# One plain chunk per feed-forward block in place of two, and the first pair's p1 and p2 among its products

## The chip, the cores and the metric

The kernel runs on one core of a Trainium2 chip. The time is the device time of one execution in microseconds (us); the median of three runs before the change is 2769.42 us (2768.85 to 2770.11). Smaller is better. Five engines work side by side, each through its own list of instructions: TensorE (PE, matrix products), VectorE (DVE), ScalarE (ACT), GpSimd (POOL) and SyncE (SP, which starts most of the loads). An instruction starts when the one ahead of it on its engine has been started and when what it reads is there.

## The reference

Two requests, of 512 and 256 tokens of 1024 numbers, go through an encoder of two layers with the same weights. Each layer is half a feed-forward block, a token mixer, and half a feed-forward block. The first layer's mixer is a gated linear recurrence in both directions, the second's is attention in a window of 128 tokens. A norm closes the trunk. The change concerns the feed-forward blocks alone, of which there are four, called f0 to f3 here:

```python
def rmsnorm(x, g):
    return x * lax.rsqrt(jnp.mean(x * x, axis=-1, keepdims=True) + NORM_EPS) * g

def swiglu_ffn(x, w1, w2):           # w1: 1024 x (2 * 2816), w2: 2816 x 1024
    gate, up = jnp.split(x @ w1, 2, axis=-1)
    return (jax.nn.silu(gate) * up) @ w2

x = x + 0.5 * swiglu_ffn(rmsnorm(x, g0), w1[0], w2[0])
x = x + mixer(rmsnorm(x, g1))
x = x + 0.5 * swiglu_ffn(rmsnorm(x, g2), w1[1], w2[1])
```

## The kernel before

All 768 tokens are handled together, as two halves of 384 (`H`). The 2816 hidden columns are 22 chunks of 128 (`NF`).

**Products in three parts.** Each fp32 operand is split in a high part (ACT rounds it by a cast) and a low part (DVE subtracts the high part from the source), in `split`. A product of two operands is then three matmuls: high by high, high by low, low by high. In `mm3` these are lines 314, 315 and 316. So the first of the three needs only the high part of the activations, the second needs their low part.

**Plain chunks and pairs.** A *plain* chunk computes gate and up by themselves: for each half, 8 slices of the input columns x 3 matmuls for the gate product, and as many for the up product, 96 matmuls in all (`up_plain`). A *pair* (`up_pair`) computes the 2 x 2 block product of (gate, up) by (first half, second half) with seven products instead of eight, p1 to p7, each 4 slices x 3 matmuls: 84 matmuls, all recorded on line 513. The price is that its operands are sums of quarters. The activations have four quarters, b00, b10, b01 and b11; the first digit is the half of the input columns (k 0 to 3, or k 4 to 7), the second is the half of the tokens. p1 uses b00, p2 uses b10, p3 uses b11. p4, p5, p6 and p7 use the factors t4, t1, t2 and t3, which are differences of quarters, formed once a block by `sums` (through `mix`, DVE lines 422, 423, 433 and 434) and split by `put` (ACT line 319, DVE line 320). The weights have sums of the same kind: POOL's queue starts accumulating DMAs for some (`into`), DVE adds others (line 215), ACT casts them (line 208 for pairs, 175 for plain chunks), and DVE makes their low parts (lines 209 and 176). Only the low part of p5's weight is made by POOL.

**A block.** Before the change, chunks 0 and 1 of each block are plain, chunks 2 to 21 are pairs. Four chunks together (two *kp* of two) make a group; their hidden values, after Silu and product, go through a seven-product scheme too, in `down_quad` (line 577). The last two chunks use plain down products.

**Entry of a block.** The normed activations must be turned so that columns lie on partitions. `turn(half, part)` does it: transposes on PE (line 385), scaled evictions on ACT (line 396), then `put` splits the quarter. The first half is turned ahead of the block. Turning the second half and forming the factors are put in a queue of steps by `later`, and `run_later` takes a step off at certain slices of the plain chunks, so these matmuls stand while the operands of the pairs are made.

**Order.** The program is written engine by engine by a scheduler that takes the order of the code as priority and sets each engine's list when the kernel is built. Weight tiles lie in pools (4 raw, 8 split), and `ahead` stages the next weights as soon as tiles come free.

Of the kernel before, what the change touches and what calls it, by code (L numbers as in the profile page):

```python
# [16 lines left out]
P = 128  # L17
# [19 lines left out]
PLAIN = 2  # L37
# [6 lines left out]
UP = ("p1", "p7", "p2", "p5", "p4", "p6", "p3")  # L44
TOK = ("p1", "p2", "p7", "p6", "p5", "p4", "p3")
# [7 lines left out]
class Trunk:  # L53
# [385 lines left out]
    def sums(self):  # L439
        for kp in range(2):  # L440
            tiles = (self.tn[(i // 2, i % 2)][:, kp] for i in range(4))
            self.mix(*tiles, lambda name, src: self.put(name, kp, src))
# [80 lines left out]
    def up_pair(self, tag, j):  # L523
        nc = self.nc
        key = (tag, j)
        a, b, c, d = (self.ps(H) for _ in range(4))
        v, w, t = (self.tmp(H) for _ in range(3))
        p = lambda name, ps, first, last: self.product(key, name, FACTOR[name], ps, first, last)
        p("p1", a, True, False)
        nc.scalar.copy(v, a)  # L530
        self.ahead()
# [3 lines left out]
        p("p2", a, False, True)  # L535
        nc.scalar.activation(a, a, AF.Silu)
        self.ahead()
# [18 lines left out]
    def down_quad(self, tag, g, hid):  # L556
        nc = self.nc
        cols = lambda b, c: self.x[b][:, c * 512 : (c + 1) * 512]
        if g == 0:
            for i in range(HB):  # L560
                x12, x21, x22 = cols(HB + i, 0), cols(i, 1), cols(HB + i, 1)
                nc.vector.tensor_add(x12, x12, x22)
                nc.vector.tensor_sub(x21, x21, x22)
# [37 lines left out]
    def ffn(self, tag, next_row):  # L601
        for g in range(GROUPS):
# [10 lines left out]
            if g == 0:  # L613
                ts = {}
                for half in range(2):
                    for j in range(PLAIN):
                        t = ts[2 * j + half] = self.up_plain(tag, j, half)
                        name = f"b{j}{half}"
                        if name != "b01":
                            put(name, t, 0)  # L620
                gather(ts, 0)
                self.run_later(len(self.deferred))
            for kp in range(2):
                if g == 0 and kp == 0:
                    continue
                ts = []
                for j in range(2):
# [932 lines left out]
```

## Time and profile before

| | |
|---|---|
| median of 3 runs | 2769.42 us |
| profiled execution, span | 2767.2 us |
| PE busy | 2745.0 us, 99%, 15117 instructions |
| DVE busy | 2206.5 us, 80%, 3766 instructions |
| ACT busy | 1386.0 us, 50%, 2589 instructions |
| POOL busy | 453.0 us, 16%, 491 instructions |
| line 513, pairs | 6720 matmuls, 1169.3 us |
| lines 314 to 316, 384 columns | 1920 matmuls, 649.9 us |
| line 577, down products | 2520 matmuls, 575.7 us |

The times of runs include some 2 us around the span that the profile shows. A row of a group gives line, engine, operation, output and inputs, the count, then busy time in us and the mean in ns, then the idle time just before and what ended it. A row of a timeline gives the start and the length in us. In the chain of waits each row is a stretch of the work that ended last. Matmuls overlap in the records: one of 384 columns is listed with 0.33 us or more, while the starts are 0.17 us apart.

### The profile page before, as it was taken

The numbers are of one execution on the slowest core, as the hardware profiler recorded it, in microseconds if no ns is written. First come the engines' busy times: TensorE is split into PE (matmuls) and PEld (weight loads), VectorE is DVE, ScalarE is ACT, GpSimd is POOL, SyncE is SP. The second block draws the span as 40 slices with busy tenths as digits, with TensorE's granted clock in tenths as the row PEclk, the third lists the DMA queues.
The fourth block names the chain that finished last, engine by engine and source line by source line (L and its number), as shares of the span: only waits on it lengthen the run. The fifth ranks groups of instructions, "written<-read, shape, count | busy, mean of one in ns | idle before, by whom it ended". The sixth has DMA issues, their size and how long they took to land.

```text
span 2767.2 us, 40933 instructions
## 1 busy us (share of the span) xinstructions
PE 2745.0 (99%) x15117; PEld 2554.8 (92%) x15117; DVE 2206.5 (80%) x3766; ACT 1386.0 (50%) x2589; POOL 453.0 (16%) x491
## 2 busy tenths in 40 slices
PE   8999999999999999999999999999999999999998
PEld 8999999989999889999999999999888889999998
DVE  8788788767887888788878887887847868788877
ACT  7344444634455675444445543444458855444443
POOL 2111121200000101211111121111105611211111
PEclk9999999999999999999999999999999999999999
DMA  6554554851122743655444355544424422655443
GB/s 172 130 125 114 126 140 124 227 161 39 39 62 66 205 119 78 143 134 131 115 117 121 78 145 134 126 119 118 130 73 111 89 69 73 145 134 130 114 118 107
DMA packets 352040, 325.22 MB, mean 118 GB/s; under 512 B 14216, under 2 KB 271200, under 8 KB 351840
## 3 DMA queue, kind: packets, MB, share of 16 engines
q1 hardware_dynamic: 303040, 224.56, 27.7%
q0 software_dynamic: 44496, 84.56, 17.4%
q10 hardware_dynamic: 4304, 13.49, 1.3%
q8 instruction: 118, 1.93, 0.3%
q14 instruction: 82, 0.67, 0.1%
HBM read 225.82 MB, written 15.73 MB: 87 GB/s over the span
## 4 chain that ended last, share of the span: by engine, by line
PE 96%; DVE 2%; ACT 1%; DMA 1%; issue 0%; DVEq 0%; POOL 0%; SPq 0%; ACTq 0%; POOLq 0%
PE ps L513 42%; PE ps L577 21%; PE ps L315 6%; PE ps L316 6%; PE ps L314 6%; PE ps L760 5%; PE ps L823 3%; PE ps L928 1%; PE ps L1414 1%; PE ps L904 1%; PE ps L385 1%; PE ps L1426 0%; PE ps L1376 0%; PE ps L1427 0%; PE ps L1377 0%; PE ps L1181 0%
## 5 line engine op out<-in xcount | busy, mean ns | idle before, releaser
L513 PE MATMUL ps<-big,w 128*128 128x384 f32 x6720 | 1169.3, 334 | 0.0
L513 PEld LDWEIGHTS ps<-big,w 128*128 128x128 f32 x6720 | 1165.9, 188 | 1.7 <-ACT tA L530 0.2
L208 ACT CAST w<-wr 128x512 fp32r<-128x512 f32 x600 | 415.8, 707 | 689.2 <-PE ps L513 274.9
L577 PE MATMUL ps<-w,big 128*128 128x512 f32 x2520 | 575.7, 390 | 0.0
L577 PEld LDWEIGHTS ps<-w,big 128*128 128x128 f32 x2520 | 472.7, 188 | 98.0 <-ACT big L319 0.4
L209 DVE TENSOR_TENSOR w<-wr,w 128x512 fp32r<-128x512 f32 (+1 forms) x520 | 438.0, 846 | 145.9 <-ACT w L208 123.9
L147 POOL DMA_DIRECT2D s<-wr x126 | 109.8, 878 | 1250.3 <-DMA s<-in_ffn_w_dram 432.0
L599 DVE SCALAR_TENSOR_TENSOR x<-ps,x 128x512 f32<-128x512 f32 x468 | 302.4, 686 | 10.1 <-PE ps L316 10.0
L314 PE MATMUL ps<-big,w 128*128 128x384 f32 x640 | 219.6, 345 | 1.2 <-ACT w L175 0.9
L315 PE MATMUL ps<-big,w 128*128 128x384 f32 x640 | 215.7, 337 | 0.7 <-DVE big L320 0.7
L316 PE MATMUL ps<-big,w 128*128 128x384 f32 x640 | 214.6, 335 | 0.0
L319 ACT CAST big<-tA 128x384 fp32r<-128x384 f32 x296 | 148.0, 513 | 115.4 <-DVE tA L545 37.0
L147 POOL DMA_DIRECT2D wr<-wr x109 | 94.9, 871 | 518.3 <-DMA wr<-in_ffn_w_dram 165.9
L760 PE MATMUL ps<-w,big 128*128 128x512 f32 x756 | 177.1, 392 | 0.1
L320 DVE TENSOR_TENSOR big<-tA,big 128x384 fp32r<-128x384 f32 x296 | 168.0, 578 | 6.7 <-ACT big L319 4.7
L209 POOL TENSOR_TENSOR w<-wr,w 128x512 fp32r<-128x512 f32 x80 | 137.4, 1718 | 197.8 <-ACT w L208 195.8
L760 PEld LDWEIGHTS ps<-w,big 128*128 128x128 f32 x756 | 140.6, 188 | 29.1 <-DVE w L320 0.6
L215 DVE TENSOR_TENSOR wr<-wr,wr 128x512 f32<-128x512 f32 (+1 forms) x120 | 123.3, 1027 | 25.9 <-issue 23.6
L314 PE MATMUL ps<-w,big 128*128 128x512 f32 x336 | 134.6, 401 | 0.1
L316 PE MATMUL ps<-w,big 128*128 128x512 f32 x336 | 131.8, 392 | 0.5 <-DVE big L400 0.5
L315 PE MATMUL ps<-w,big 128*128 128x512 f32 x336 | 131.8, 392 | 0.0
L315 PEld LDWEIGHTS ps<-big,w 128*128 128x128 f32 x640 | 120.6, 188 | 2.0 <-DVE big L320 1.7
(214 smaller groups left out, 3504.0 us busy)
## 6 DMA issues: line engine op xcount, KB each, us to landing
wr<-in_ffn_w_dram SPq DMA_DIRECT2D x264, 512.0 KB, 4.0
s<-wr POOLq DMA_DIRECT2D x126, 256.0 KB, 4.8
s<-in_ffn_w_dram SPq DMA_DIRECT2D x120, 256.0 KB, 3.2
wr<-wr POOLq DMA_DIRECT2D x80, 256.0 KB, 3.8
wr<-in_hg_w_in_dram SPq DMA_DIRECT2D x32, 512.0 KB, 3.9
wr<-wr POOLq DMA_DIRECT2D x29, 512.0 KB, 4.6
spill<-x ACTq DMA_DIRECT2D x12, 512.0 KB, 4.0
kept<-big POOLq DMA_DIRECT2D x8, 768.0 KB, 9.7
```

The costliest lines, as they stand in the source:

```text
L147: self.nc.gpsimd.dma_start(out, src, accum_op=ALU.add)
L208: nc.scalar.copy(h, src)
L209: (eng or nc.vector).tensor_sub(l, src, h.bitcast(F32))
L314: nc.tensor.matmul(out, a[0], b[0], start=first, stop=False)
L315: nc.tensor.matmul(out, a[0], b[1], start=False, stop=False)
L316: nc.tensor.matmul(out, a[1], b[0], start=False, stop=last)
L319: self.nc.scalar.copy(hi, src)
L320: self.nc.vector.tensor_sub(lo, src, hi.bitcast(F32))
L513: self.nc.tensor.matmul(ps, a[x], b[y], start=first and k == 0 and i == 0, stop=k == 3 and i == 2, skip_group_check=True,)
L577: nc.tensor.matmul(ps, a[x], w[y], start=name == chain and kp == 0 and q == 0, stop=kp == 1 and q == 2, skip_group_check=True,)
L599: self.nc.vector.scalar_tensor_tensor(x, ps, c, x, ALU.mult, ALU.add)
L760: nc.tensor.matmul(ps, x[:, sl], y, start=fresh and k == 0 and q == 0, stop=k == 3 and q == 2, skip_group_check=True,)
```

## The change

Each block has one plain chunk (`PLAIN = 1`), and chunk 1 becomes the second member of a first pair of chunks, computed with seven products. For the first half of the tokens, the block does the plain chunk's gate product, then p1 of chunk 1, then the plain chunk's up product (with `run_later` at its slices 2 and 6), then p2 of chunk 1, then what is left of the queue of steps, the sums. The plain chunk's second half follows, and then p7, p5, p4, p6 and p3. The weights of that chunk are staged in this order (`UP_OPEN`). `sums` forms each factor over both halves of the columns before it forms the next: t3, t1, t2's difference, t4, and t2's split last. The six additions on x ahead of the first down product (lines 562 and 563 before) are held until the first pair's last DVE instruction. At the last down products the weights are released without staging ahead each time; that is done once behind them.

```diff
-PLAIN = 2
+PLAIN = 1
+UP_OPEN = ("p1", "p2", "p7", "p5", "p4", "p6", "p3")
...
     def sums(self):
-        for kp in range(2):
-            tiles = (self.tn[(i // 2, i % 2)][:, kp] for i in range(4))
-            self.mix(*tiles, lambda name, src: self.put(name, kp, src))
+        b11, b12, b21, b22 = (self.tn[(i // 2, i % 2)] for i in range(4))
+
+        def form(name, t, a, b):
+            for kp in range(2):
+                self.nc.vector.tensor_sub(t[:, kp], a[:, kp], b[:, kp])
+            return lambda: [self.put(name, kp, t[:, kp]) for kp in range(2)]
+
+        form("t3", b22, b12, b22)()
+        form("t1", b12, b11, b12)()
+        t2 = form("t2", b11, b11, b22)
+        form("t4", b21, b21, b11)()
+        t2()
...
-                self.plan_quad((tag, i), (gate, up), (NC, P), UP)
+                self.plan_quad((tag, i), (gate, up), (NC, P), UP_OPEN if i == PLAIN else UP)
...
-    def up_plain(self, tag, j, half):
+    def up_plain(self, tag, j, half, between=None):
         pss = []
         for c in range(2):
+            if c and between:
+                between()
             wh, wl = self.take((tag, j, c))
...
-                if half == 0 and k in (((), (2, 6)), ((3, 7), (3, 7)))[j][c]:
+                if half == 0 and c and k in (2, 6):
                     self.run_later()
...
+    def up_first(self, tag, j):
+        a, v = self.ps(H), self.tmp(H)
+        self.product((tag, j), "p1", FACTOR["p1"], a, True, False)
+        self.nc.scalar.copy(v, a)
+        self.ahead()
+        return a, v
+
+    def up_second(self, tag, j, a):
+        self.product((tag, j), "p2", FACTOR["p2"], a, False, True)
+        self.nc.scalar.activation(a, a, AF.Silu)
+        self.ahead()
+
-    def up_pair(self, tag, j):
+    def up_pair(self, tag, j, opened=None):
...
+        a, v = opened or self.up_first(tag, j)
...
+        if not opened:
+            self.up_second(tag, j, a)
...
         if g == 0:
-            for i in range(HB):
-                x12, x21, x22 = cols(HB + i, 0), cols(i, 1), cols(HB + i, 1)
-                nc.vector.tensor_add(x12, x12, x22)
-                nc.vector.tensor_sub(x21, x21, x22)
+            with self.tc.issue_after(self.begun):
+                for i in range(HB):
+                    x12, x21, x22 = cols(HB + i, 0), cols(i, 1), cols(HB + i, 1)
+                    nc.vector.tensor_add(x12, x12, x22)
+                    nc.vector.tensor_sub(x21, x21, x22)
...
+                begin = g == 0 and kp == 0
+                if begin:
+                    opened = []
+                    keep(self.up_plain(tag, 0, 0, lambda: opened.extend(self.up_first(tag, 1))), 0)
+                    self.up_second(tag, 1, opened[0])
+                    self.run_later(len(self.deferred))
+                    keep(self.up_plain(tag, 0, 1), 0)
+                for j in range(begin, 2):
+                    for t in self.up_pair(tag, 4 * g + 2 * kp + j, opened if begin else None):
+                        keep(t, j)
                 gather(ts, kp)
+                if begin:
+                    self.begun = self.last_dve
...
-                    self.done((tag, "last", c))
+                    self.release((tag, "last", c))
...
+        self.ahead()
```

The scheduler's lists show where this puts things. The changed kernel's line numbers are 1 to 24 higher (315 for 314, 320 and 321 for 319 and 320, 445 for the subtractions of `sums`, 525 for 513).

First, PE at the start of f1, where the gate product of chunk 0 begins. Before (ps_9264 is its output and ps_9289 that of the up product; big_9194 and big_9197 are b00, its first and its second two slices; L385 are transposes of the second half's tokens):

```order
L385 MATMUL ps_9237<-ident_r,big_9109 128x128
L314 MATMUL ps_9264<-big_9194,w_9115 128x384
L314 MATMUL ps_9289<-big_9194,w_9140 128x384
L385 MATMUL ps_9299<-ident_r,big_9134 128x128
L385 MATMUL ps_9299<-ident_r,big_9167 128x128
L385 MATMUL ps_9305<-ident_r,big_9134 128x128
L385 MATMUL ps_9305<-ident_r,big_9167 128x128
L315 MATMUL ps_9264<-big_9194,w_9115 128x384
L316 MATMUL ps_9264<-big_9194,w_9116 128x384
...
L316 MATMUL ps_9264<-big_9197,w_9116 128x384
L315 MATMUL ps_9289<-big_9194,w_9140 128x384
```

And after (ps_9280 is the gate product, big_9213 and big_9216 are b00, big_9261 and big_9264 are b10, L525 on ps_9305 is p1):

```order
L386 MATMUL ps_9256<-ident_r,big_9128 128x128
L315 MATMUL ps_9280<-big_9213,w_9134 128x384
L316 MATMUL ps_9280<-big_9213,w_9134 128x384
...
L316 MATMUL ps_9280<-big_9216,w_9134 128x384
L317 MATMUL ps_9280<-big_9216,w_9135 128x384
L315 MATMUL ps_9280<-big_9261,w_9134 128x384
L316 MATMUL ps_9280<-big_9261,w_9134 128x384
...
L317 MATMUL ps_9280<-big_9264,w_9135 128x384
L525 MATMUL ps_9305<-big_9213,w_9267 128x384 x6
L525 MATMUL ps_9305<-big_9216,w_9267 128x384 x6
```

Before, the up product's matmuls on b00 and some transposes came ahead of the gate product's on b10; now the gate product's 24 matmuls stand in a row, with b10 from the 13th on, and p1 behind them.

Second, DVE in f1 from the low part of b11 on. Before (big_9359 and big_9362 are b11's low parts; L422, L423, L433 and L434 form the factors of the first two slices, and big_9394 is t4's low part of these):

```order
L320 TENSOR_TENSOR big_9359<-big_9342,big_9359 128x2x384
L320 TENSOR_TENSOR big_9362<-big_9342,big_9362 128x2x384
L422 TENSOR_TENSOR big_9342<-big_9303,big_9342 128x768
L505 TENSOR_TENSOR tA_9368<-tA_9368,ps_9289 128x384
L423 TENSOR_TENSOR big_9303<-big_9177,big_9303 128x768
L320 TENSOR_TENSOR big_9371<-tA_9368,big_9371 128x384
L433 TENSOR_TENSOR big_9177<-big_9177,big_9342 128x768
L320 TENSOR_TENSOR big_9389<-big_9303,big_9389 128x2x384
L434 TENSOR_TENSOR big_9225<-big_9225,big_9177 128x768
...
L320 TENSOR_TENSOR big_9394<-big_9225,big_9394 128x2x384
```

And after (big_9394 and big_9397 are b11's low parts, big_9427 and big_9430 t3's, big_9435 and big_9438 t1's, big_9445 is the first of t4's; the two L210 make low parts of the weights of p6 and p3):

```order
L321 TENSOR_TENSOR big_9397<-big_9377,big_9397 128x2x384
L321 TENSOR_TENSOR big_9406<-tA_9403,big_9406 128x384
L210 TENSOR_TENSOR w_9422<-wr_8976,w_9422 128x512
L445 TENSOR_TENSOR big_9377<-big_9338,big_9377 128x768 x2
...
L321 TENSOR_TENSOR big_9430<-big_9377,big_9430 128x2x384
L445 TENSOR_TENSOR big_9338<-big_9196,big_9338 128x768
L321 TENSOR_TENSOR big_9435<-big_9338,big_9435 128x2x384
...
L321 TENSOR_TENSOR big_9438<-big_9338,big_9438 128x2x384
L445 TENSOR_TENSOR big_9244<-big_9244,big_9196 128x768 x2
L210 TENSOR_TENSOR w_9482<-wr_8976,w_9482 128x512
L321 TENSOR_TENSOR big_9445<-big_9244,big_9445 128x2x384
```

Between b11's and t4's first low part there were five subtractions of factors and one low part, of t1; now there are eight subtractions, four low parts of t3 and t1, and two splits of weights.

Third, PE where that t4 is read, after the change (ps_9496 is the last of the plain chunk's second half; L525 on ps_9531 with big_9427 is p7, on ps_9532 p5, on ps_9531 with big_9445 p4, on ps_9530 p6):

```order
L317 MATMUL ps_9496<-big_9397,w_9160 128x384
L525 MATMUL ps_9531<-big_9427,w_9273 128x384 x6
L525 MATMUL ps_9531<-big_9430,w_9273 128x384 x6
L525 MATMUL ps_9532<-big_9435,w_9276 128x384 x6
L525 MATMUL ps_9532<-big_9438,w_9276 128x384 x6
L525 MATMUL ps_9531<-big_9445,w_9320 128x384 x6
L525 MATMUL ps_9531<-big_9448,w_9320 128x384 x6
L525 MATMUL ps_9530<-big_9451,w_9422 128x384 x6
```

48 matmuls of the plain chunk's second half and the 24 of p7 and p5 stand ahead of p4; before, 96 of two plain chunks' second halves stood ahead of the first pair's p1.

More of the change, by code (lines that the diff above doesn't have):

```diff
@@ L521, in product @@
         self.release((*key, name))
-    def up_pair(self, tag, j):
+    def up_first(self, tag, j):
[9 more added lines that the diff above has]
+    def up_pair(self, tag, j, opened=None):
         nc = self.nc
         key = (tag, j)
-        a, b, c, d = (self.ps(H) for _ in range(4))
-        v, w, t = (self.tmp(H) for _ in range(3))
+        a, v = opened or self.up_first(tag, j)
+        b, c, d = (self.ps(H) for _ in range(3))
+        w, t = (self.tmp(H) for _ in range(2))
         p = lambda name, ps, first, last: self.product(key, name, FACTOR[name], ps, first, last)
-        p("p1", a, True, False)
-        nc.scalar.copy(v, a)
-        self.ahead()
         p("p7", c, True, False)
@@ L534, in up_pair @@
         self.ahead()
-        p("p2", a, False, True)
-        nc.scalar.activation(a, a, AF.Silu)
-        self.ahead()
+        if not opened:
+            self.up_second(tag, j, a)
         p("p5", d, True, False)
```

23 lines of the change are left out of this document (5 added, 18 removed).

## The prediction

> **What bounds the kernel now.** I read the page first (engines, then the chain), then the list of waits of TensorE (PE), then the timeline of the places where a feed-forward block begins.
>
> ```profile
> span 2767.2 us, 40933 instructions
> PE 2745.0 (99%) x15117; PEld 2554.8 (92%) x15117; DVE 2206.5 (80%) x3766; ACT 1386.0 (50%) x2589; POOL 453.0 (16%) x491
> PE 96%; DVE 2%; ACT 1%; DMA 1%; issue 0%; DVEq 0%; POOL 0%; SPq 0%; ACTq 0%; POOLq 0%
> PE ps L314 <- ACT w L175: 0.9, 1, 0.9
> PE ps L315 <- DVE big L320: 0.7, 2, 0.3
> ```
>
> PE is busy 99% of the span and makes 96% of the chain. The last two rows (total us, times, longest) are the waits of the plain chunks: under 1 us each. So the time is the number of matmuls plus what PE is made to wait, and a change that removes matmuls gains only as long as PE doesn't outrun the engines that prepare its operands. Two rows price a matmul:
>
> ```profile
> L513 PE MATMUL ps<-big,w 128*128 128x384 f32 x6720 | 1169.3, 334 | 0.0
> 1062.91 29.12 PE ps L513 x168
> ```
>
> 29.12/168 = 0.1733 us, and 1169.3/6720 = 0.174. Durations in a timeline overlap their neighbours by about 0.1 us, so below I take differences of starts.
>
> **What is removed.** Per block a plain chunk of 96 matmuls becomes a pair of 84: 12 fewer, 48 in four blocks, 48 x 0.174 = **-8.35 us**. What it adds elsewhere (44 DVE subtractions, 28 ACT casts, 8 accumulating DMAs on POOL's queue) is weight staging for one more pair, and is covered where DVE and ACT run ahead of PE; with no cover at all the price would be 44 x 0.6 = 26 us of DVE work, but DVE is idle for 20% of the span. The other edits of the weights' order (p2 before p7, `release` with one `ahead` at the end) move casts among themselves by less than one 0.5 us cast: nothing. The waits of PE below are where I expect it to pay.
>
> **Term 1: b10 at the gate product.** f1's entry; PE, then ACT, then DVE:
>
> ```profile
> 1027.33 0.44 PE L315 MATMUL ps<-big,w 128*128 128x384 f32 x1 [0.34 <-DVE big L320]
> 1026.51 1.06 ACT L175 CAST w<-wr 128x1024 fp32r<-128x1024 f32 x1
> 1027.46 1.08 ACT L364 ACTIVATE big<-x 128x1024 f32<-128x1024 f32 x1
> 1029.16 1.53 ACT L396 ACTIVATE big<-ps,cols 128x384 f32<-128x384 f32 x3
> 1030.55 1.59 ACT L319 CAST big<-big 128x768 fp32r<-128x768 f32 x2
> 1031.84 1.82 DVE L320 TENSOR_TENSOR big<-big,big 128x768 fp32r<-128x768 f32 x2
> 1043.15 0.84 ACT L319 CAST big<-big 128x768 fp32r<-128x768 f32 x1
> ```
>
> At 1027.33 PE's second matmul of the block has b00's low part. Before, the up product's matmuls on b00 then filled the time until b10's high part (ACT, cast from 1030.55) and low part (DVE, from 1031.84) were there. Now the 24 matmuls of the gate product stand in a row. The 13th, first on b10, is reached at 1027.33 + 11 x 0.1733 = 1029.24, and the 14th, which reads the low part, at 1029.41. On ACT the cast of chunk 1's weight at 1026.51 goes (0.95), so the cast of b10 starts at 1029.60; its first half takes 0.84, and the low part 0.95: 1031.4. The wait is **2.0**. It is 0 if ACT drew level, and 2.9 if that 0.95 weren't won back.
>
> f2 in the same way, where two such casts stood ahead:
>
> ```profile
> 1517.06 0.44 PE L315 MATMUL ps<-big,w 128*128 128x384 f32 x1
> 1518.20 1.06 ACT L175 CAST w<-wr 128x1024 fp32r<-128x1024 f32 x1
> 1521.18 1.60 ACT L319 CAST big<-big 128x768 fp32r<-128x768 f32 x2
> ```
>
> Low part at 1521.18 - 1.9 + 0.84 + 0.95 = 1521.07; PE at 1517.06 + 12 x 0.1733 = 1519.14: **1.9**. In f3 other matmuls do stand between, so nothing. Together **+3.9** (0 to 5.8).
>
> **Term 2: t4 at product p4.** The time is counted from the end of p1, for f1 to f3.
>
> ```profile
> 55.72 0.47 ACT L530 COPY tA<-ps 128x384 f32<-128x384 f32 x1
> 1050.29 0.62 ACT L208 CAST w<-wr 128x512 fp32r<-128x512 f32 x1 [1.71 <-PE ps L315]
> 1039.81 1.28 ACT L504 ACT_TABLE_LOAD   x1
> 1041.10 0.49 ACT L504 ACTIVATE tA<-ps 128x384 f32<-128x384 f32 x1
> 1032.95 2.03 ACT L396 ACTIVATE big<-ps,cols 128x384 f32<-128x384 f32 x4
> 1034.82 1.62 ACT L319 CAST big<-big 128x768 fp32r<-128x768 f32 x2
> 1036.28 2.05 ACT L396 ACTIVATE big<-ps,cols 128x384 f32<-128x384 f32 x4
> 1039.09 1.83 DVE L320 TENSOR_TENSOR big<-big,big 128x768 fp32r<-128x768 f32 x2 [1.52 <-ACT big L319]
> 1044.41 0.95 DVE L320 TENSOR_TENSOR big<-big,big 128x768 fp32r<-128x768 f32 x1
> 1045.28 0.95 DVE L434 TENSOR_TENSOR big<-big,big 128x768 f32<-128x768 f32 x1
> 1058.31 0.69 DVE L209 TENSOR_TENSOR w<-wr,w 128x512 fp32r<-128x512 f32 x1
> ```
>
> ACT: copy of p1 0.37, weight cast 0.53, table load 1.29, Silu 0.39, four evictions 1.87, two casts 1.46, four evictions 1.90 (each its row less the overlap of 0.1). b11's cast begins at 7.8 and its first half is there at 8.65. DVE then makes both low parts (2 x 0.87) until 10.4, a hidden half's low part 0.47, a weight split 0.60, and 12 operations of 768 columns at 0.87 (1045.28 - 1044.41), which form t3, t1, t2 and t4 and write low parts of t3 and t1: 21.9. t4's high cast (0.84) is done at 22.75, and its first low part 0.9 later: 23.65. PE meanwhile does 24 matmuls of the up product (4.16), 24 transposes at 0.1 (2.4), p2 (2.08), half 1's 48 (8.33), p7 and p5 (4.16), and p4's first (0.17): 21.3. It waits 2.3, less 0.1 for its changes between transposes and matmuls: **2.2** a block, 6.6 in three. Bounds per block: 0 if ACT gains 2 us on my list (the table load and the weight cast are 1.8 of it, and may be served before p1 ends), and 3.6 if another 1.4 of weight work slips in.
>
> f0 differs: its order puts the second four evictions behind a Silu that waits for p2's end. From there the list is 0.39 + 0.53 + 1.87 + 0.84 + 0.05 to b11's low part at 3.7, 1.74, 10.44, 0.60, 0.9 = 17.3; PE's is 12 transposes 1.2, 8.33, 4.16, 0.17 = 13.9: **3.4** (2 to 5). Term 2 is **+10.0** (2 to 16).
>
> **Term 3: f0's start.**
>
> ```profile
> 14.79 0.45 PE L315 MATMUL ps<-big,w 128*128 128x384 f32 x1
> 19.11 0.52 ACT L365 ACTIVATE stat<-stat,eps 128x1 f32<-128x1 f32 x2
> 25.07 0.44 PE L314 MATMUL ps<-big,w 128*128 128x384 f32 x1 [0.93 <-ACT w L175]
> ```
>
> The gate product ends at 14.79 + 23 x 0.1733 = 18.8. p1's weight is cast after the statistics at 19.11: 19.3 + 0.5 = 19.8, a wait of 1.0 (0 to 3, as its load may land later than ACT is free). The wait of 0.93 for chunk 1's weights at 25.07 goes. **+0.1** (-1 to 2).
>
> **Term 4: the first down product.**
>
> ```profile
> 1092.03 28.60 PE ps L577 x126
> 1093.67 0.55 DVE L320 TENSOR_TENSOR big<-tA,big 128x384 fp32r<-128x384 f32 x1
> 1083.80 1.23 DVE L209 TENSOR_TENSOR w<-wr,w 128x1024 fp32r<-128x1024 f32 x1 [2.59 <-ACT w L208]
> 1031.24 0.69 DVE L562 TENSOR_TENSOR x<-x 128x512 f32<-128x512 f32 x1
> ```
>
> Its second product, 18 matmuls of 0.227 after 1092.03, is at 1096.1; its b10 is done at 1094.2: 1.9 of slack. The six additions on x now stand on DVE within the second pair: 6 x 0.6 = 3.6. DVE's idle times there (2.59 and three smaller ones of about 1) take most of it, not all, and staging is later, since one more pair has passed through POOL's queue. I take a quarter of what the 3.6 exceeds 1.9 as a wait, **0.5** a block, **+2.0** (0, all in the gaps, to 4 x 1.7 = 6.8).
>
> **Term 5: POOL against DVE.**
>
> ```profile
> 45.31 8.12 POOL L209 TENSOR_TENSOR w<-wr,w 128x512 fp32r<-128x512 f32 x1 [9.24 <-ACT w L208]
> 1072.02 1.60 POOL L209 TENSOR_TENSOR w<-wr,w 128x512 fp32r<-128x512 f32 x1
> 1071.97 2.21 DVE L209 TENSOR_TENSOR w<-wr,w 128x512 fp32r<-128x512 f32 x1 [0.16 <-ACT w L208]
> ```
>
> POOL splits p5's weight. Where DVE ran without a gap it took 8.12; where it got in, DVE's split took 2.21 in place of 0.69, 1.5 more. The change sets one more pair's split per block beside the DVE run of term 2. One hit in four blocks is **+1.5** (0 to 4 x 1.5 = 6). [...]
>
> **Sum:** -8.35 + 3.9 + 10.0 + 0.1 + 2.0 + 1.5 = +9.15. The profiled span 2767.2 becomes 2776.4. The median of the runs is 2769.4, 2.2 above the span, for what lies around it: **2778.6 us, taken as 2779**, 0.3% slower.
>
> **Rivals.**
> (a) *The waits are covered.* Tile order isn't time: ACT and DVE are 50% and 80% busy, and if they draw ahead by 2 us at each entry, terms 1, 2 and 4 go, the 0.93 with them: 2769.4 - 8.35 - 0.9 = 2760. For it speaks that before's entries waited under 1 us in spite of similar lists; against it, that DVE was busy for the whole of f0's start (row under (d)) and that half 1's cover is cut from 96 matmuls to 48. It decides if p4 waits under 0.3.
> (b) *It cancels.* Term 1 stays at 3.9 and p4 waits about 1 us a block, since the table load and the weight cast on ACT are served before p1 ends (1.8 of the 2.2 saved in f1 to f3, 1.4 of the 3.4 in f0), terms 3 and 5 come to nothing, and term 4 stays: -8.35 + 3.9 + 1.2 + 2.0 + 2.0 = +0.75, 2770.
> (c) *DVE is the bound.* POOL's split stops DVE inside each block's run (term 5 at 6) and the added staging makes the down product wait in full (term 4 at 6.8): +9.15 + 4.5 + 4.8 = +18.5, 2788. For it, the 2.21; against it, DVE's idle 2.59 after the first pair.
> (d) *The clock.* f0's start in a table of busy time by stretch (length, then busy us and instructions of PE, PEld, DVE, ACT, POOL, then the granted clock, the DMA share and GB/s):
>
> ```profile
> 14.00:60.00 46.00, 45.07 (x264) 44.20 (x263) 46.00 (x69) 36.30 (x62) 13.03 (x7) 1.00 0.60 150
> ```
>
> The clock is 1.00 there, and no wait inside it passes 1 us. f0's waits of 3.4 would be the longest. If the clock halved for a stretch of 20 matmuls after it, 20 x 0.17 = 3.5 us more: 2782. [...]
>
> **How the numbers follow.** The forecast has 0.55, with its own range 2774 to 2784; (a) 0.10, (b) 0.17, (c) 0.12, (d) 0.06. The range 2764 to 2788 leaves out most of (a) and the upper end of (c). A difference under 0.2%, 5.5 us, is no change: below 2763.9 is faster, above 2774.9 slower. Faster: (a), **0.10**. Same: (b) and the low edge of the forecast, 0.17 + 0.05 = **0.22**. Slower: the rest, **0.68**.
>
> **What would show it.** In the new profile: 384 fewer plain matmuls of 384 columns and 336 more in products; PE's row for the gate product's second-half matmul in f1 and f2 with an idle time of about 2 us, released by DVE's low part; at p4 of each block's first pair 2 to 3.5 us, released by the same line; a down product that waits 0 to 1.7. If p4 doesn't wait, term 2 is wrong and the result is (a) or (b); a DVE split over 2 us inside the sums is (c); a granted clock below 0.99 in a slice after f0's start is (d).

## The result: slower by 1.1%, three times what was forecast

The changed kernel takes 2799.82 us (median of 4 runs, 2798.01 to 2800.4), the kernel before 2769.25 in the same comparison. The ratio is 1.0111, 95% interval 1.0099 to 1.0123. The forecast was 2779 with a range to 2788: the sign was right, the size was not. The profiled span grew from 2767.2 to 2796.2, by 29.0 us.

The page of the changed kernel: span, engines' busy time, and the chain of waits by engine.

```profile
span 2796.2 us, 40956 instructions
PE 2751.4 (98%) x15069; PEld 2556.3 (91%) x15069; DVE 2227.6 (80%) x3810; ACT 1393.1 (50%) x2615; POOL 476.6 (17%) x503
PE 88%; DVE 6%; ACT 3%; DMA 2%; issue 1%; POOL 0%; SPq 0%; DVEq 0%; ACTq 0%; POOLq 0%
```

The waits of PE in the changed kernel, in the blocks (total us, times, longest):

```profile
PE ps L599 <- DVE x L621: 7.8, 4, 2.3
PE ps L525 <- ACT big L320: 5.0, 4, 2.5
PE ps L525 <- DVE big L321: 4.1, 4, 1.0
PE ps L315 <- ACT big L320: 4.1, 4, 1.4
PE ps L316 <- DVE big L321: 3.3, 7, 0.9
PE ps L525 <- ACT w L209: 1.3, 1, 1.3
```

PE has 48 matmuls fewer (15069 against 15117) and yet is busy 6.4 us longer. DVE's and ACT's share of the chain went from 3% to 9%. The six rows of waits are 25.6 us, where the same lines of the kernel before had 1.8; all but 0.3 us of either lies in the feed-forward blocks (the 0.3 is in the first mixer, at 518.54 and at 506.94).

The waits are not all of it. A table of consecutive stretches of f1 around p4 of the first pair (length, then busy us and instructions of PE, PEld, DVE, ACT and POOL, then the granted clock, DMA share, GB/s):

```profile
1065.44:1068.85 3.41, 3.22 (x19) 2.90 (x17) 3.41 (x5) 1.95 (x5) 1.15 (x1) 1.00 0.00 0
1068.85:1072.26 3.41, 1.75 (x8) 1.49 (x9) 3.41 (x5) 3.31 (x5) 3.41 (x1) 1.00 0.22 60
1072.26:1075.68 3.42, 3.42 (x13) 3.42 (x12) 3.42 (x6) 0.00 (x0) 3.42 (x1) 0.50 0.31 94
1075.68:1079.09 3.41, 3.41 (x21) 3.41 (x21) 3.41 (x7) 0.93 (x2) 1.62 (x2) 1.00 0.66 146
```

In the second row PE is busy for 1.75 of 3.41 us, as it waits at p4. In the third it never waits, but its clock is 0.50, and it does 13 matmuls where the row behind it has 21. Seven such stretches lie in the blocks, none before the change, and each is 3.41 us long: 7 x 3.41 x 0.5 = 11.9 us, an estimate that takes PE as busy throughout (it was in six of them, and 91% in the seventh). So 25.6 - 1.8 of waits + 11.9 of clock - 8.35 of removed matmuls is 27.4 of the 29.0 measured; 1.6 is not attributed.

### The profile page after: what moved, and what is told of

Its sections match the earlier page's. It is cut to its first block, busy times and chain, and to the rows that moved or that the text cites. A ratio compares the mean times of both kernels' runs of the same rounds, so it can differ in the third digit from the quotient of the medians.

```text
span 2796.2 us, 40956 instructions
## 1 busy us (share of the span) xinstructions
PE 2751.4 (98%) x15069; PEld 2556.3 (91%) x15069; DVE 2227.6 (80%) x3810; ACT 1393.1 (50%) x2615; POOL 476.6 (17%) x503
## 3 DMA queue, kind: packets, MB, share of 16 engines
q0 software_dynamic: 45648, 86.66, 17.5%
## 4 chain that ended last, share of the span: by engine, by line
PE 88%; DVE 6%; ACT 3%; DMA 2%; issue 1%; POOL 0%; SPq 0%; DVEq 0%; ACTq 0%; POOLq 0%
PE ps L525 39%; PE ps L599 20%; PE ps L784 5%; PE ps L316 5%; PE ps L317 5%; PE ps L315 5%; PE ps L847 3%; DVE big L321 2%; DVE big L445 1%; DMA wr<-in_ffn_w_dram 1%; DVE w L210 1%; PE ps L952 1%; ACT big L397 1%; PE ps L1438 1%; DMA wr<-wr 1%
## 5 line engine op out<-in xcount | busy, mean ns | idle before, releaser
L525 PE MATMUL ps<-big,w 128*128 128x384 f32 x7056 | 1237.5, 335 | 10.4 <-ACT big L320 5.0
L525 PEld LDWEIGHTS ps<-big,w 128*128 128x128 f32 x7056 | 1230.3, 189 | 14.8 <-ACT big L320 6.3
L209 ACT CAST w<-wr 128x512 fp32r<-128x512 f32 (+1 forms) x624 | 430.3, 704 | 684.5 <-PE ps L525 257.6
L210 DVE TENSOR_TENSOR w<-wr,w 128x512 fp32r<-128x512 f32 (+1 forms) x540 | 441.6, 822 | 148.7 <-ACT w L209 135.0
L621 DVE SCALAR_TENSOR_TENSOR x<-ps,x 128x512 f32<-128x512 f32 x468 | 301.7, 681 | 10.8 <-PE ps L317 10.0
L210 POOL TENSOR_TENSOR w<-wr,w 128x512 fp32r<-128x512 f32 x84 | 151.4, 1802 | 223.0 <-ACT w L209 222.8
L315 PE MATMUL ps<-big,w 128*128 128x384 f32 x512 | 178.7, 350 | 4.1 <-ACT big L320 4.1
L316 PE MATMUL ps<-big,w 128*128 128x384 f32 x512 | 174.0, 340 | 3.3 <-DVE big L321 3.3
L317 PE MATMUL ps<-big,w 128*128 128x384 f32 x512 | 172.8, 338 | 0.0
L216 DVE TENSOR_TENSOR wr<-wr,wr 128x512 f32<-128x512 f32 (+1 forms) x124 | 130.5, 1052 | 19.9 <-issue 18.2
L321 DVE TENSOR_TENSOR big<-big,big 128x768 fp32r<-128x768 f32 (+2 forms) x106 | 90.9, 894 | 26.3 <-ACT big L320 26.2
```

Source lines behind the costliest of these rows:

```text
L209: nc.scalar.copy(h, src)
L210: (eng or nc.vector).tensor_sub(l, src, h.bitcast(F32))
L315: nc.tensor.matmul(out, a[0], b[0], start=first, stop=False)
L316: nc.tensor.matmul(out, a[0], b[1], start=False, stop=False)
L317: nc.tensor.matmul(out, a[1], b[0], start=False, stop=last)
L321: self.nc.vector.tensor_sub(lo, src, hi.bitcast(F32))
```

## Where the time went, place by place

Timeline of PE in f1 (start, length, then the idle time just before and what ended it): first the gate product's b00 and b10, then p4 of the first pair, then the first down product.

```profile
1038.44 0.44 PE L316 MATMUL ps<-big,w 128*128 128x384 f32 x1 [0.55 <-DVE big L321]
1042.02 0.44 PE L315 MATMUL ps<-big,w 128*128 128x384 f32 x1 [1.39 <-ACT big L320]
1043.02 0.44 PE L316 MATMUL ps<-big,w 128*128 128x384 f32 x1 [0.55 <-DVE big L321]
1069.48 0.45 PE L525 MATMUL ps<-big,w 128*128 128x384 f32 x1 [0.82 <-ACT big L320]
...
1114.29 3.89 PE L599 MATMUL ps<-w,big 128*128 128x512 f32 x16 [2.17 <-DVE x L621]
```

b10's wait is 1.39 + 0.55 = 1.94 in f1 (forecast 2.0), and the same in f2 (forecast 1.9). At p4 PE waits 0.82 for t4's high part and, one matmul later, 1.03 for its low part: 1.85 (forecast 2.2). f0's p4 waits 2.54 + 1.03 = 3.57 (forecast 3.4). The down product's wait of 2.17 is the one that was missed, and its releaser isn't the one that was named: DVE's L621, which adds p1's product from its bank to x, and not b10. In the kernel the second product accumulates onto that same bank; its first matmul began at 1114.29, 0.15 behind L621's end (1113.46 + 0.68).

What makes L621 late can be followed through six rows of f1's timeline (DVE, SP's queue, POOL, ACT, DVE, DVE):

```profile
1095.67 1.28 DVE L210 TENSOR_TENSOR w<-wr,w 128x512 fp32r<-128x512 f32 x2
1096.98 0.37 SPq L161 DMA_DIRECT2D wr<-in_ffn_w_dram  x1
1101.40 0.87 POOL L148 DMA_DIRECT2D wr<-wr  x1 [11.67 <-DMA wr<-in_ffn_w_dram]
1106.71 2.00 ACT L209 CAST w<-wr 128x1024 fp32r<-128x1024 f32 x2 [6.52 <-DMA wr<-wr]
1107.80 1.23 DVE L210 TENSOR_TENSOR w<-wr,w 128x1024 fp32r<-128x1024 f32 x1 [3.10 <-ACT w L209]
1113.46 0.68 DVE L621 SCALAR_TENSOR_TENSOR x<-ps,x 128x512 f32<-128x512 f32 x1
```

A weight of the down product was loaded late: SP started the load right behind two weight splits on DVE, which were over at 1096.95, and 10.9 us ahead of the down product (1107.84). So POOL started the accumulating DMA at 1101.40, 6.4 us ahead. ACT could cast the weight only at 1106.71. DVE, whose next instruction splits it, stood idle for 3.10 us, with seven operations on the pair's hidden values, one more weight split and L621 queued behind. The six additions on x were over by then, at 1104.70. In the kernel before, PE's timeline has the down product start at 1091.87; the corresponding load started at 1076.85, 15.0 us ahead, and the DMA at 1081.30, 10.6 us ahead:

```profile
1076.85 0.37 SPq L160 DMA_DIRECT2D wr<-in_ffn_w_dram  x1
1081.30 0.87 POOL L147 DMA_DIRECT2D wr<-wr  x1 [7.68 <-DVE w L209]
1094.61 0.68 DVE L599 SCALAR_TENSOR_TENSOR x<-ps,x 128x512 f32<-128x512 f32 x1
```

There the row that answers to L621 began at 1094.61 and was over by 1095.3, and the second product's first matmul began at 1095.99. So the real slack was 0.7 us, not the 1.9 that the forecast counted to b10. L621 began 2.74 us after the down product's start before the change and 5.62 after it; these 2.88 us less the slack of 0.7 are the wait of 2.17.

The load's lead goes with the wait in every profile. In the 64 blocks of the 16 kernels of this case, PE waits 1.48 us or more at this place wherever the last such load leads the down product by 10.9 us or less (40 blocks), 0 to 1.5 where it leads by 11.3 to 12.3 (9 blocks), and not at all where it leads by 12.8 or more (15 blocks). In the changed kernel it is 10.9 in all four blocks, before it 14.4 to 15.0.

## Experiments

All times below are compared with the kernel before on the same chip; spans are those of the profiled execution, 2796.2 for the changed kernel and 2767.2 for the one before. A span is that of one execution, and the runs of one kernel lie 1 to 4 us apart (8 in `b00_first_slices`), so spans that differ by less than that tell nothing by themselves. First theory: waits of PE for operands that DVE and ACT prepare too late, each followed by half clock where it empties a stretch. Rivals: the clock falls for another reason; the down product waits for the additions on x, for POOL, or for the hidden values; the sums' order is at fault by itself.

### Dummy matmuls in the wait at p4

```diff
+        if opened:
+            pw = self.take((*key, "p4"))
+            for k in range(4):
+                q = self.operand("b00", k)
+                for x, y in ((0, 0), (0, 1), (1, 0)):
+                    nc.tensor.matmul(b, pw[x][:, k, :], q[y], start=True, stop=True, skip_group_check=True)
         p("p4", c, False, True)
```

> Twelve matmuls whose result nobody reads (p4's weight by b00, into the bank that p6 overwrites) stand ahead of p4 in each block's first pair: 48 matmuls more than in the changed kernel. Theory (the wait at p4 lets a window of the clock gate run half empty, and the next 3.4 us go at half clock): the dummies fill the 1.85 us of wait in f1 to f3 and 2.1 of the 3.6 in f0, the four half-clock stretches behind p4 go, 4 x 1.7 = 6.8 us: span 2796.2 - 6.8 = 2789.4 in spite of more work, and the half-clock stretches fall from 7 to 3. Rival (the clock has another cause than PE's idleness, or the stretches cost nothing): span 2796 to 2798, stretches still 7.

2789.25 us, ratio 1.0075 (1.0060 to 1.0090), span 2787.2: 9.0 us less than the changed kernel, with 48 more matmuls. PE's timeline at p4 of f1 (L567 are the dummies):

```profile
1064.09 2.24 PE L567 MATMUL ps<-big,w 128*128 128x384 f32 x12
1066.17 6.05 PE L525 MATMUL ps<-big,w 128*128 128x384 f32 x32
```

The table of busy time for the two stretches around it:

```profile
1064.64:1068.06 3.42, 3.37 (x19) 3.05 (x18) 3.42 (x5) 3.12 (x5) 3.42 (x1) 1.00 0.28 81
1068.06:1071.47 3.41, 3.41 (x22) 3.41 (x21) 3.41 (x7) 0.00 (x0) 3.41 (x1) 1.00 0.26 78
```

p4 no longer waits after the dummies, and the clock stays at 1.00. The half-clock stretches fell from 7 to 1. Useless work at full clock costs less here than a wait that leaves a stretch about half empty (PE was busy for 1.75 of 3.41 us there in the changed kernel, and is for 3.37 of 3.42 now), and the mean granted clock goes from 0.995 to 0.999: in these two profiles the clock follows PE's idleness. More stretches went than forecast, since f0's wait at the down product (2.35 us, as long as in the changed kernel) and f2's entry escaped theirs too; that part is luck.

### The additions on x at the block's entry

```diff
-            with self.tc.issue_after(self.begun):
+            with nullcontext():
```

> The six additions on x ahead of the first down product are no longer held until the first pair's last DVE instruction. My term 4 (the additions load DVE in the second pair): the waits of the first down product, 7.8 us in sum, fall to under 2, and f0's half-clock stretch behind it goes (1.7): span about 2788. Rival (the down weights are staged late, because raw buffers and POOL's queue came free late; the additions are hidden): the 7.8 stay within 1 us, span 2795 to 2798.

2790.30 us, ratio 1.0076 (1.0059 to 1.0092), span 2788.4. The row of waits that the experiment was about stands as it was:

```profile
PE ps L599 <- DVE x L621: 7.7, 4, 2.3
```

So the additions are not what delays the down product, and that part of term 4 falls. The 7.8 us gained lie elsewhere: 3 half-clock stretches in place of 7 (6.8 us), and shorter waits at the entry, where the scheduler now places other instructions.

### p5's low part on DVE

```diff
-            split(name, own[name], nc.gpsimd if up and name == "p5" else None)
+            split(name, own[name], nc.gpsimd if up and name == "p5" and order is not UP_OPEN else None)
```

> The low part of p5's weight in each block's first pair is made by DVE and no longer by POOL, where it took 8.76 us in f1 beside a DVE without gaps and held up the accumulating DMA queued behind it. If that delay is what makes the down weights late: waits of the first down product fall from 7.8 to 2 or less, and p4's rise by 0.6 a block (one more split ahead of t4), span about 2793. Rival (the raw tiles come free late, since the weight splits of the first pair stand behind the sums on DVE): the down waits stay at 7 to 9, span 2796 to 2800.

2796.19 us, ratio 1.0098 (1.0083 to 1.0113), span 2795.9. The down product's waits are 7.8 again, as the rival had it. The span fell by 0.3 us and the median by 3.6, with intervals that overlap, so no gain is shown. POOL's split did take 8.76 us in f1 of the changed kernel, and a DMA issue stood behind it, but the chain to the down product doesn't pass there:

```profile
1067.70 8.76 POOL L210 TENSOR_TENSOR w<-wr,w 128x512 fp32r<-128x512 f32 x1 [12.85 <-ACT w L209]
1076.41 0.89 POOL L148 DMA_DIRECT2D wr<-wr  x1
```

### The sums in their old order, in the changed kernel and the other way round

The first kernel puts the old `sums` (by slices) in the changed kernel. The second puts the new `sums` (factor by factor) in the kernel before, and nothing else.

```diff
-        form("t3", b22, b12, b22)()
-        form("t1", b12, b11, b12)()
-        t2 = form("t2", b11, b11, b22)
-        form("t4", b21, b21, b11)()
-        t2()
+        for kp in range(2):
+            tiles = (self.tn[(i // 2, i % 2)][:, kp] for i in range(4))
+            self.mix(*tiles, lambda name, src: self.put(name, kp, src))
```

> The sums are formed as before the change, first both pairs' slices 0 and 1 of all four factors, then slices 2 and 3; all else as in the changed kernel. Theory (DVE's run behind b11 is the limit): p7 needs t3 for slices 2 and 3, which is now the 15th of DVE's 16 operations, at 10.4 + 1.1 + 15 x 0.87 = 24.5 after p1, and PE is there at 18.3: about 6 us of wait at p7 in place of 1.85 at p4, +4 us a block, and a half-clock stretch as now: span about 2812. Rival (the new order of the sums costs or brings nothing): span within 2 us of 2796.

2788.59 us, ratio 1.0072 (1.0057 to 1.0087), span 2786.2. I expected 2812, and both readings were wrong. Its waits of PE, and one row of its timeline of DVE in f1:

```profile
PE ps L516 <- ACT big L320: 10.7, 4, 3.7
PE ps L590 <- DVE x L612: 1.3, 2, 1.0
```

```profile
1063.46 0.68 DVE L210 TENSOR_TENSOR w<-wr,w 128x512 fp32r<-128x512 f32 x1
```

PE waits at p7 for t3, 2.24 us in f1 and not 6, since the scheduler had taken most of the subtractions first and most of the low parts after. In the changed kernel p4 took 1.85 there (9.1 in the four blocks, against 10.7), so the two orders cost about the same. But the half-clock stretches fell from 7 to 4, and the down product's waits from 7.8 to 1.3: the last weight split of the first pair stands between the sums, at 1063.46. In the changed kernel it stands behind all of the subtractions (its timeline of DVE, then of SP's queue):

```profile
1069.35 0.68 DVE L210 TENSOR_TENSOR w<-wr,w 128x512 fp32r<-128x512 f32 x1
...
1070.10 0.37 SPq L161 DMA_DIRECT2D wr<-in_ffn_w_dram  x1
```

That split frees a raw weight tile, and SP's next load of a pair's weights starts right behind it, at 1070.10. With the sums by slices it starts at 1064.22, 40.0 us ahead of the down product and not 37.7.

> The kernel before with one part of the change alone, the sums formed factor by factor. There 96 matmuls of the second half and the pair's p1 stand ahead of the first factor's use, so nothing waits: span 2767.2 within 1 us. Rival (the new order delays weight splits behind it on DVE, as in the changed kernel): 2770 or more, with a wait at the first down product.

2768.82 us, ratio 0.9999 (0.9990 to 1.0009), span 2767.4. With two plain chunks ahead, the new order costs nothing. It is no fault by itself; it costs where fewer matmuls stand ahead of the first use.

### The first pair without low parts of its weights

```diff
-                (eng or nc.vector).tensor_sub(l, src, h.bitcast(F32))
+                if eng or order is not UP_OPEN:
+                    (eng or nc.vector).tensor_sub(l, src, h.bitcast(F32))
             view = lambda t: t.rearrange("p (a b) -> p a b", a=4 if up else 2)
-            self.staged[(*key, name)] = (view(hi), view(lo), 1 if up else 2)
+            self.staged[(*key, name)] = (view(hi), view(lo if eng or order is not UP_OPEN else hi), 1 if up else 2)
```

> The changed kernel without DVE's low parts of the first pair's weights (six splits a block; p5's, on POOL, stays): the matmuls read the high part in their place, so the products of this pair lack a small term. PE's order is the same. Theory (the raw tiles come free late since these splits queue behind the sums on DVE): loads for the second pair and the down product start several us earlier, the down product's waits fall from 7.8 to under 3, p4's by 0.6 a block, and with f0's clock stretch at the down product the span is 2782 to 2789. Rival (the hidden values of the second pair are late by themselves): the down waits stay above 6, span 2791 to 2794 from p4 alone.

2782.48 us, ratio 1.0048 (1.0033 to 1.0063), span 2780.4: 15.8 us less. Six DVE instructions of 0.6 us a block are gone. The third matmul of each product now reads the high part of the weight again, so the pair's main term is counted twice, where I had written that a small term is lacking. The kernel leaves out part of the work, and only its time is of use. Its waits of the blocks, the five largest rows:

```profile
PE ps L526 <- DVE big L322: 4.1, 4, 1.0
PE ps L316 <- ACT big L321: 4.1, 4, 1.4
PE ps L526 <- ACT big L321: 3.2, 4, 2.5
PE ps L317 <- DVE big L322: 3.0, 7, 0.6
PE ps L526 <- ACT w L209: 1.2, 1, 1.2
```

There is no row for the down product: its 7.8 us are gone altogether, with the operations on the hidden values unchanged. p4's wait fell by 0.6 in f1 to f3, as forecast for one split less ahead of t4, and the half-clock stretches are 3. So the DVE work that the added pair brings is what makes the down product late: 7.8 of waits, 1.8 at p4 and 4 x 1.7 of clock are 16.4, against the 15.8 measured. Of the ways in which this work delays the down product, the late release of raw tiles fits the loads' starts: the down weight's load leads by 12.8 us here in all four blocks, and by 10.9 in the changed kernel. That the tiles alone, without DVE's shorter queue, would do it was not separated.

### Other orders at the block's start

If only places were wrong, another order should bring the gain of 8.35 us. Eight kernels try it. In `quarters` the plain products go by quarters: gate on b00, p1, up on b00, then gate and up on b10, the gate product on b10 held back by an order on the instructions.

```diff
+        for part in range(2):
+            for c in range(2):
+                wh, wl = ws[c]
+                with self.tc.issue_after(last) if last and not c else nullcontext():
+                    for k in range(4 * part, 4 * part + 4):
...
+                if not part and not c:
+                    between()
```

> The changed kernel, with the first half's plain products by quarters: gate product on b00, p1, up product on b00, and only then gate and up on b10, held there by an order on the instructions. So 36 matmuls (6.2 us) stand ahead of b10 where 12 did. Theory (term 1): the waits of 1.94 for b10 in f1 and f2 go, and f2's half-clock stretch behind it: span 2796.2 - 3.9 - 1.7 = 2790.6, with the waits at p4 and at the down product as they are. Rival (what ACT loses elsewhere comes back at p4): span within 2 us of 2796.

2797.82 us, ratio 1.0106 (1.0091 to 1.0121), span 2797.8. The span is within 2 us of 2796, as the rival had it, though not for its reason. b10's waits in f1 and f2 are gone, and p1's weight is late in their place (8.3 us in sum), since ACT casts it behind b10:

```profile
1043.07 0.62 PE L546 MATMUL ps<-big,w 128*128 128x384 f32 x2 [2.62 <-ACT w L209]
```

In `turns_early` the second half's turns stand ahead of p1 and at slice 0 of the up product.

```diff
             if c and between:
+                self.run_later()
                 between()
...
-                if half == 0 and c and k in (2, 6):
+                if half == 0 and c and k == 0:
```

> The changed kernel, with the second half's turns taken from the queue ahead of p1 and at slice 0 of the up product, in place of slices 2 and 6 of it. ACT then evicts and casts b01 and b11 ahead of the table load and the Silu, some 3 to 4 us earlier as seen from PE. Theory (term 2: the chain from b11 to t4 is late by 1.85 us, and 3.6 in f0, and lets a window run half empty): p4's waits go in f1 to f3, at least half of f0's, and three or four half-clock stretches: -5.5 - 2 - 6 = about 2783. Rival (DVE's sums are bound by what stands behind them and not by b11): p4 waits as before, span 2794 to 2797.

2785.19 us, ratio 1.0062 (1.0046 to 1.0079), span 2782.5, as expected. p4 waits no more in f1, f2 and f3, its waits fall from 9.1 to 2.3 in sum, and three half-clock stretches are left of seven. DVE begins b11's low parts at 1051.21 in f1 where it was 1056.11. Term 2's mechanism is thereby shown: b11 earlier, t4 in time. The size of the gain isn't all p4's: b10's wait in f1 fell too (1.94 to 1.04), while f0's waits grew at p1 (1.3 to 2.6) and came up at p2 (2.8).

Two runs join the edits: quarters with early turns, and these with the sums by slices.

> Both edits together: plain products by quarters, and the turns at slices 0 and 2 of the up product on b00. Sum of the two by my theory: 2796.2 - 5.6 - 13.5 = 2777, with the down product's waits of 7.8 left. Rival (the two use the same ACT time): 2783 or more.

2792.94 us (1.0074 to 1.0104), span 2790.5.

> Both edits, and the sums formed by slices as before the change, which left 1.3 us of the 7.8 at the down product, as the weight splits stand between the sums and free the raw tiles some 2 us earlier. Theory: 2777 - 6.5 - 1.7 = 2769, and p7's wait for t3 (2.2 in f1 with the sums by slices) is covered by the earlier start. Rival (p7 waits as it did there, 10.7 in sum): 2778 or more.

2790.33 us (1.0065 to 1.0095), span 2788.9. Both missed what I expected, and the rivals' figures came true, the second's not by its condition: p7 waits 3.2 us in sum and not 10.7. PE waits for p1's weight, which ACT casts late, in both (8.5 and 8.2 us in sum). `b00_first` removes that: gate and up on b00, gate on b10, p1, up on b10.

```diff
+TURNS = ((0, 1, 3), (1, 0, 6))
...
+        for part, c in ((0, 0), (0, 1), (1, 0), (1, 1)):
...
+            if part and not c:
+                between()
```

> The changed kernel with another order at a block's start: gate and up on b00 (24 matmuls, as before the change), gate on b10, then p1, then up on b10, then p2; the second half's turns are taken at the up product's slice 3 on b00 and the gate product's slice 6. p1's weight, for which the order by quarters waited 2.6 us, is now needed 24 matmuls later. Theory (each wait is a matter of what stands ahead of it, and each emptied window costs 1.7 more): b10's, p1's and p4's waits go in f1 to f3, p4's in f0 falls under 1.5; the down product's 7.8 falls to 3 to 6, since the sums end some 5 us earlier and free the raw tiles; at most 2 half-clock stretches. Span 2767 to 2775. Rival (a fixed supply of ACT and DVE work per block is what PE waits for, and a wait that goes at one place comes back at the next, as in the order by quarters): 2782 or more.

2790.54 us (1.0064 to 1.0092), span 2788.8. b10's wait and p1's are gone in f1 to f3. p4's has come back (1.27 in f1, and 1.63 in f3), and the down product's waits are 8.4: the rival's 2782 or more.

> The same with the sums by slices as before the change. If the weight splits between the sums are what the down product needs, its waits fall to 0 to 2 and the span is 3 to 5 us below that of b00_first; p7's wait for t3 stays under 1 with the earlier start. Rival: the sums' order doesn't matter once they start early; within 2 us of b00_first.

2800.24 us (1.0098 to 1.0126), span 2800.4, no faster than the changed kernel: 10.4 us at the down product, 7.0 for the part of a weight that POOL makes, and 9 half-clock stretches. Neither case I wrote down came true.

> b00_first without holding back the six additions on x. In the changed kernel their release left the down product's waits at 7.7 and gave 7.8 us elsewhere (waits of the entry and 4 half-clock stretches). If that gain was the entry's, which b00_first already has: within 2 us of b00_first. If the additions delay the down product after all: 2 to 5 us below it.

2786.75 us (1.0049 to 1.0074), span 2782.4; two half-clock stretches are left of five, but 7.9 us at the down product. The median fell by 3.8 us and the span by 6.4. This is neither of the two cases I wrote down, since the additions still don't delay the down product: in the profiles it is three stretches of clock (5.1) and shorter waits in f0.

> turns_early without holding back the additions on x. Each alone brought the span to 2782.5 and 2788.4, largely by the same waits (b10 and p4). If they add where they differ (the two half-clock stretches left in turns_early, b10's 1.04 in f1): 2778 to 2781. If DVE's supply up to p4 is what binds: 2782 to 2786, the waits moving to another place.

2783.88 us (1.0034 to 1.0067), span 2783.5: two edits that each gained don't add up: the ratio is 1.0050 where `turns_early` alone has 1.0062, and the intervals overlap. The figure is the one that the rival named, a bound by DVE's supply, and a table of busy time agrees with it. The table has f1 from its first matmul on, first the kernel before (to the first pair's p1), then `b00_first_adds` (to p4's low part):

```profile
1025.90:1062.90 37.00, 36.62 (x217) 36.12 (x218) 33.02 (x44) 27.49 (x46) 6.14 (x3) 1.00 0.25 58
...
1034.70:1064.70 30.00, 28.50 (x169) 27.66 (x169) 28.45 (x39) 27.34 (x48) 4.51 (x3) 1.00 0.20 45
```

In the 30 us up to p4, PE has 28.50 us of work, DVE 28.45 and ACT 27.34. Before, DVE had 33.02 of 37.00, 4 us to spare; now 1.5. With three engines nearly level, an order that frees one place is likely to load another, as the eight orders did; that no order would do better is not shown. No kernel tried is faster than the one before.

## Why the prediction was wrong, by its own steps

**The removed work** (-8.35): 48 matmuls fewer, as the instruction counts say. Right, but 'busy' went up by 6.4, with the 11.9 of clock set against the 8.35.

**Term 1** (b10, +3.9): f1 1.94 and f2 1.94, forecast 2.0 and 1.9; f3 nothing. Right. But the same two lines also wait in f0, 1.12 + 0.87 = 2.0 us, where half 1's first quarter is read, which I had left out, and 1.26 at b00 in f1 to f3, 0.55 of it there before. With these and the 0.3 in the mixer the two lines wait 7.4, 6.5 beyond before's.

**Term 2** (t4, +10.0): 9.1 measured, 1.85 a block and 3.57 in f0. Right in place, releaser and size; the run with early turns shows the mechanism.

**Term 3** (f0's start, +0.1): p1's weight took 1.3 and not 1.0, and 0.9 went. Right.

**Term 4** (the down product, +2.0, bounds 0 to 6.8): 7.8, beyond its upper bound. This is the first step that failed. I measured slack to b10, 1.9 us, where the matmul that waits needs DVE's addition from the bank ahead of it, with 0.7 of slack. I charged the additions on x, and their release left 7.7; what makes it late is the first pair's weight splits, as the run without them shows. The later staging was named in passing and not priced: the weight's load leads by 10.9 us in place of 15.0.

**Term 5** (POOL against DVE, +1.5): it went the other way. POOL lost (8.76 us), and moving its work to DVE left the down product's waits at 7.8 and gained nothing clear of noise. In the sum it should have been nothing. The 8.76 stood beside a DVE without a gap. In the forecast's own row of 2.21 DVE began at 1071.97 and POOL at 1072.02, and there it was DVE that took longer, against POOL's 1.60. Each of the two was thus seen to take longer beside the other; what decides which is not shown.

**Rival (d), the clock** (3.5 us, chance 0.06): this is the second step that failed, and the larger. It should have been no rival but a term: 7 stretches, 11.9 us. A stretch costs 1.7 us, by the estimate of 3.41 x 0.5, and not the 3.5 of the forecast; their number is what was missed. No run shows the forecast's 20 matmuls at half clock: behind p4 of f1, 13 ran in the 3.42 us at 0.50. I reckoned with one stretch, behind the longest wait, 3.4 us in f0, and let shorter waits pass as harmless; in f1 1.66 us without PE work within one stretch, the one with p4's wait, stood ahead of the stretch at 0.50.

With the terms as measured, 23.8 of waits beyond before's and 11.9 of clock stand where the forecast had 17.5 for both. From the forecast's 9.15, the clock adds 11.9, term 4 5.8, term 1's lines 2.6 and term 3 0.3, while term 2 takes off 0.9 and term 5 1.5: 27.4 of the 29.0, as above. Terms 1 to 3 came near by the waits that they name; that the errors of terms 1, 2 and 5 nearly cancel is luck.

## What the runs showed of the hardware

In the changed kernel's profile the recorded granted clock is 1.00 or 0.50, and each of the seven stretches at 0.50 in the blocks lasts 3.413 us. The first recorded stretch at 1.00 begins at 14.13 us, and every border behind it lies at a whole multiple of 3.413 us from there. In the 3.41 us ahead of the seven, PE was busy for 0.44 to 1.75 us, 13 to 51%. Of the stretches of that grid that were followed by full clock again, the one with the least had 1.95 us (57%, at 2369.33). At p4 of f1 a wait of 1.85 us thus cost about 3.6 in all, with the estimate of 1.7 for the stretch behind it. The grid doesn't lie the same in both profiles: before the change the first recorded stretch at 1.00 begins at 15.03 us. A grid that also shifts among the runs of one kernel would fit their spread where there are such waits, but no run shows it directly; in `b00_first_slices` the two longest have a mean clock of 0.994 and the two shortest 0.996. Where a wait fell in the grid mattered, too. Rows of the changed kernel's f1 show a longer wait than p4's, 2.17 us at the down product, split by a border so that PE is busy for 2.31 and 2.35 us of the two stretches, with the clock staying at 1.00:

```profile
1109.81:1113.22 3.41, 2.31 (x11) 1.57 (x9) 3.41 (x7) 0.99 (x2) 0.00 (x0) 1.00 0.00 0
1113.22:1116.64 3.42, 2.35 (x10) 1.99 (x11) 3.42 (x7) 2.07 (x4) 0.00 (x0) 1.00 0.52 153
1116.64:1120.05 3.41, 3.41 (x16) 2.82 (x15) 3.41 (x8) 1.54 (x3) 0.00 (x0) 1.00 0.00 0
```

## What to carry to other kernels

With PE at 99%, a removed matmul was worth 0.17 us here, and the cover that it gave to other engines may be worth more: count the work of DVE and ACT up to the first place where PE needs their product, before and after, and compare it with PE's own. Price a wait with what it did to the clock, here 1.7 us for each of the seven stretches at 0.50, and look at the busy share of the stretch in which it falls (13 to 51% ahead of these) and not at its length alone. And take the slack ahead of a matmul from the releaser that the profile names, banks included, and not from the operand that one has in mind.
